# Four splits and four gate products of a state-space output, issued slot by slot

## The chip, the cores and the metric

The kernel runs on one core of a Trainium2 chip. The metric is the time of one execution on the device in microseconds (us), taken as the median over runs; beside it stands the profile of one execution, from which all rows below come.

## The reference

Two layers of a decoder trunk are applied to an input of 512 tokens by 1024 channels, in float32. In each layer the normalised input `h` goes through one large projection whose columns feed three token mixers, their gates and three merge gates. What matters here is the third mixer, a state-space model (SSM) over 512 channels, whose output `y` passes a gated linear unit and is multiplied with its own gate:

```python
h = rmsnorm(x, norm_g)
proj = h @ w_in
...
y = jax.nn.gelu(y)
y_ssm = y * jax.nn.sigmoid(y @ w_glu + b_glu)
...
y_c = y_ssm * jax.nn.silu(cz)
merged = sigmoid(ga) * (y_a @ proj_a) + sigmoid(gb) * (y_b @ proj_b) + sigmoid(gc) * (y_c @ proj_c)
x = x + merged @ w_out
```

## The kernel before, in words

**Three products for one.** The large matrix products are made with operands split in two: `split` (L280) lets ScalarE round a float32 tile to the matmul type (`h`, line L284) and VectorE subtract that from the original to give the low half (`l`). `three` issues high by high, high by low and low by high, and sums them in PSUM. Weights are treated alike: class `Weights` loads units of 128 by 1024 from HBM on the SP queue (`raw`, L308); `make` rounds a unit on ScalarE (`wh`, L318) and makes its low half on VectorE (`wl`). Raw units and both halves share twelve tiles, so a new half waits until TensorE or VectorE has let an older tile go.

**Slots.** The order of the work is a list of pieces, `ORDER`; each is one slot, and `now` counts them. A piece of a token-major product (`rq`, `rk`, `rv0`, `rv1`) is 24 matmuls for 128 tokens that use four weight units in turn, six matmuls a unit; four pieces share the four units. Other work is written as generators that yield the number of slots until their next step. In each slot the program issues the steps that are due, then the piece's matmuls, then steps that asked to come behind them, and then `W.fill()`, which makes the next weight units as tiles allow. After the last piece of a token-major product it makes four units at once. Every engine runs its own instructions in the order in which they were issued.

**Around the change.** The generator `ssm(q)` computes one quarter of the SSM's output, tile `y`, kept as `g[q]`. When the fourth quarter is done, in the third of the four pieces of `rv0`, it waits one slot and then splits all four tiles: four roundings `gh` on ScalarE and four subtractions `gl` on VectorE, in the slot of the last piece of `rv0`. Two slots later (`K["s7"]`) GpSimd multiplies each tile in place with the gate `zc`, named `silu` in the trace. The halves are read by the stage `glu`, which comes right after `rv1`; its evacuation multiplies the tiles, by then multiplied with the gate, with the sigmoid. The other names in the rows: `rv` (L1167) are the evacuations of `rv0` and `rv1`, one per piece; `rT` (L1160) copies a transposed piece of `rk` out of PSUM; `m` are the rotary products of `rk`; `kts` is the retention mixer's first work on GpSimd after `rv1`.

```python
            if q == 3:
                yield 1
                for i in range(4):
                    gs[i] = split(g[i], "g")
                yield K["s7"]
                for i in range(4):
                    while zc[i] is None:
                        yield 1
                    GT(out=g[i], in0=g[i], in1=zc[i], op=ALU.mult)
```

Of the kernel before, what the change touches and what calls it, by code (L numbers as in the profile page):

```python
# [14 lines left out]
ALU = mybir.AluOpType  # L15
# [20 lines left out]
K = dict(  # L36

    nw=12, w=4, raw=4, b=48,

    sb0=0, sb_gap=4, ssm0=6, ssm_gap=3, ret0=9, ret_gap=3, x0=-3, x1=2, ret_pre=4, lead=9,  # L40

    g=0.9, v=0.7,

    n1=1, n2=1, q1=1, q2=1, k1=1, k2=2, s1=1, s2=1, s3=1, s4=2, s5=1, s6=1, s7=2, b1=1, b2=1, b3=1,
# [142 lines left out]
def trunk(ctx: ExitStack, tc, x_in, w_in, par_in, bc_in, ng_in, cst_in, rope_in, out):  # L187
# [3 lines left out]
    def counted(f, engine, each):  # L191


        def g(*a, **k):
            o = k["out"] if "out" in k else a[0]
            load[engine] += 0.07 * (engine != "T") + each * math.prod(o.shape[1:])
            return f(*a, **k)  # L197

        return g
# [4 lines left out]
    GT, GS = counted(nc.gpsimd.tensor_tensor, "G", 2.2e-3), counted(nc.gpsimd.tensor_scalar, "G", 1.2e-3)  # L204
# [11 lines left out]
    def bt(name, dt=F32, shape=(P, 512)):  # L216
        return bp.tile(list(shape), dt, tag="b", name=name)
# [7 lines left out]
    def psm(name):  # L225
        return ps_sm.tile([P, 512], F32, tag="sm", name=name)
# [14 lines left out]
    def C(n):  # L241
# [7 lines left out]
        out=negm, in_=negm, pattern=[[1, P]], base=0, channel_multiplier=-1, compare_op=ALU.is_ge, fill=0.0  # L249
# [31 lines left out]
    def split(src, name, shape=(P, 512)):  # L281
        h = bt(name + "h", F32R, shape)
        l = bt(name + "l", F32R, shape)
        ACT(h, src, AF.Copy)  # L284
        TT(out=l, in0=src, in1=h.bitcast(F32), op=ALU.subtract)
        return h, l
# [108 lines left out]
    def transposed(src):  # L395
        pt = psm("T4")
        for i in range(4):
            nc.tensor.transpose(pt[:, i * P : i * P + P], src[:, i * P : i * P + P], ident)  # L398
        return pt
# [235 lines left out]
    def v3(ap, n=32):  # L635
        return ap.rearrange("p (g m) -> p g m", m=n)
# [173 lines left out]
    def layer(l, last, base):  # L810
# [59 lines left out]
        g = [None] * 4  # L870

        def ssm(q):
            win, ca, mt, T = coef.q[q]
            p0 = G * l + 8 * q

            pu = transposed(U[q])
            yield 0
            ut = bt("ut")
            for k in range(2):
                src = pu[64 * k : 64 * k + 64].rearrange("p (i c j) -> p i c j", i=4, j=2)  # L880
                for j in range(2):
                    dst = ut[64 * j : 64 * j + 64].rearrange("p (i k c) -> p i k c", i=4, k=2)
                    ACT(dst[:, :, k, :], src[:, :, :, j], AF.Copy)
            yield K["s1"]
            ps = psm("S")
            for n in range(8):
                sl = slice(n * 64, n * 64 + 64)
                MM(ps[:, sl], win[n // 4][:, n % 4 * P : n % 4 * P + P], ut[:, sl], start=True, stop=True)
            yield 0

            H, tm, tx = bt("H"), bt("tm"), bt("tx")
            lo, hi = slice(0, 64), slice(64, P)
            TT(out=tm, in0=ps, in1=T[0], op=ALU.mult)
            TT(out=tx[lo], in0=ps[hi], in1=T[1][hi], op=ALU.mult)
            TT(out=tx[hi], in0=ps[lo], in1=T[1][lo], op=ALU.mult)
            yield K["s2"]
            TT(out=tm, in0=tm, in1=tx, op=ALU.add)
            for n in range(8):
                sl = slice(n * 64, n * 64 + 64)
                nc.vector.tensor_tensor_scan(  # L900
                    tm[:, sl], r8[:, p0 + n : p0 + n + 1].to_broadcast([P, 64]), tm[:, sl], 0.0, ALU.mult, ALU.add
                )
            nc.gpsimd.memset(v3(H, 64)[:, :, 0:1], 0.0)
            yield K["s3"]

            def sh0(ap):
                return v3(ap, 64)[:, :, 0:63]

            def sh1(ap):
                return v3(ap, 64)[:, :, 1:64]  # L910


            TT(out=sh1(H), in0=sh0(tm), in1=sh0(T[0]), op=ALU.mult)
            TT(out=sh0(tx)[lo], in0=sh0(tm)[hi], in1=sh0(T[1])[hi], op=ALU.mult)
            TT(out=sh0(tx)[hi], in0=sh0(tm)[lo], in1=sh0(T[1])[lo], op=ALU.mult)
            TT(out=sh1(H), in0=sh1(H), in1=sh0(tx), op=ALU.subtract)
            yield K["s4"]

            py = psm("py")
            for i in range(4):  # L920

                for part in range(2):
                    for n in (i, i + 4):
                        sl = slice(n * 64, n * 64 + 64)
                        o = py[64 * (n // 4) : 64 * (n // 4) + 64, n % 4 * P : n % 4 * P + P]
                        k = 2 * (n % 2) + n // 4
                        if part == 0:
                            MM(o, ut[:, sl], mt[n % 4 // 2][:, k * P : k * P + P], start=True, stop=False)
                        else:
                            MM(o, H[:, sl], ca[:, n, 1:9, :].rearrange("p a b -> p (a b)"), start=False, stop=True)  # L930
            coef.used = q + 1
            yield 0
            ysb = bt("ysb")
            ACT(
                ysb.rearrange("p (j g m) -> p g j m", j=8, g=4), py.rearrange("p (g j m) -> p g j m", g=4, j=8), AF.Copy
            )
            yield K["s5"]
            pt = transposed(ysb)
            yield 0
            y = bt("y")  # L940
            for k in range(2):
                src = pt[64 * k : 64 * k + 64].rearrange("p (i h c) -> p i h c", i=4, h=2)
                for h in range(2):
                    dst = y[64 * h : 64 * h + 64].rearrange("p (c i k) -> p i c k", i=4, k=2)
                    ACT(dst[:, :, :, k], src[:, :, h, :], AF.Copy)

            u, sg = bt("gu"), bt("gs")
            ACT(u, y, AF.Square, scale=math.sqrt(0.044715))
            yield K["s6"]
            STT(out=u, in0=u, scalar=1.0, in1=y, op0=ALU.add, op1=ALU.mult)  # L950
            yield 0
            ACT(sg, u, AF.Sigmoid, scale=2.0 * math.sqrt(2.0 / math.pi))
            TT(out=y, in0=y, in1=sg, op=ALU.mult)
            g[q] = y
            if q == 3:
                yield 1
                for i in range(4):
                    gs[i] = split(g[i], "g")
                yield K["s7"]
                for i in range(4):  # L960
                    while zc[i] is None:
                        yield 1
                    GT(out=g[i], in0=g[i], in1=zc[i], op=ALU.mult)


        gs, yc, yb, mg, ya = [None] * 4, [None] * 4, [None] * 4, [None] * 8, [None] * 8
        zc, zb = [None] * 4, [None] * 4
# [349 lines left out]
        def quarters():  # L1317

            q = len(starts) - 1
            if q < 4 and coef.ready >= q and now[0] >= starts[-1]:  # L1320
                spawn(ssm(q), now[0])
                starts.append(now[0] + K["ssm_gap"])
# [15 lines left out]
        for name, m in mains:  # L1338
            i = now[0]
# [22 lines left out]
    while due:  # L1362
        i = min(due)
# [28 lines left out]
```

## Time and profile before

| what | value |
|---|---|
| median of 3 runs | 1310.49 us (1309.92 to 1311.5) |
| the profiled execution | 1311.17 us |
| its span, first to last instruction | 1309.5 us |
| TensorE busy | 97% |
| VectorE, ScalarE, GpSimd busy | 65%, 41%, 29% |
| mean granted clock of TensorE | 0.992 |

The profiled execution gives every duration and wait used below. PE is TensorE, DVE VectorE, ACT ScalarE, POOL GpSimd and SP the engine that issues the loads. Times in a timeline count from the start of the span. A matmul is pipelined: its row says 0.39 us, while the next starts 0.23 us after it.

### The profile page before, as it was taken

The numbers are of one execution on the slowest core, as the hardware profiler recorded it, in microseconds if no ns is written. First come the engines' busy times: TensorE is split into PE (matmuls) and PEld (weight loads), VectorE is DVE, ScalarE is ACT, GpSimd is POOL, SyncE is SP. The second block draws the span as 40 slices with busy tenths as digits, with TensorE's granted clock in tenths as the row PEclk, the third lists the DMA queues.
The fourth block names the chain that finished last, engine by engine and source line by source line (L and its number), as shares of the span: only waits on it lengthen the run. The fifth ranks groups of instructions, "written<-read, shape, count | busy, mean of one in ns | idle before, by whom it ended". The sixth has DMA issues, their size and how long they took to land. (4 is left out here: it accounts for less than half of the span.)

```text
span 1309.5 us, 16640 instructions
## 1 busy us (share of the span) xinstructions
PE 1271.7 (97%) x6360; PEld 1048.5 (80%) x6360; DVE 855.6 (65%) x1189; ACT 537.6 (41%) x919; POOL 382.5 (29%) x452
## 2 busy tenths in 40 slices
PE   6989989999999999999999999899999999999998
PEld 5867768788887888888888877788888878888887
DVE  5997678776785438556365576789657844575542
ACT  5445534445343534332244445344534534423311
POOL 3340036638442012000042000584555311210000
PEclk9989989999999999999999999899999999999999
DMA  6232221222322322234433222122241232222342
GB/s 223 90 124 77 65 65 49 81 81 89 119 68 65 104 77 77 81 97 141 161 118 127 81 65 71 43 81 65 84 127 65 65 120 90 65 74 88 97 135 75
DMA packets 37375, 120.05 MB, mean 92 GB/s; under 512 B 4144, under 2 KB 4528, under 8 KB 37296
## 3 DMA queue, kind: packets, MB, share of 16 engines
q1 hardware_dynamic: 29664, 105.40, 25.2%
q10 hardware_dynamic: 7632, 13.59, 3.1%
q8 instruction: 50, 0.82, 0.3%
q14 instruction: 29, 0.24, 0.1%
HBM read 114.78 MB, written 4.19 MB: 91 GB/s over the span
## 5 line engine op out<-in xcount | busy, mean ns | idle before, releaser
L197 DVE TENSOR_TENSOR wl<-raw,wh 128x1024 fp32r<-128x1024 f32 x196 | 251.6, 1294 | 114.6 <-ACT wh L318 111.8
L197 PE MATMUL mm<-hh,wh 128*128 128x512 f32 x640 | 256.0, 400 | 0.0
L197 PE MATMUL mm<-hh,wl 128*128 128x512 f32 x640 | 251.2, 393 | 4.9 <-DVE wl L197 4.9
L197 PE MATMUL mm<-hl,wh 128*128 128x512 f32 x640 | 250.7, 392 | 0.0
L318 ACT ACTIVATE wh<-raw 128x1024 fp32r<-128x1024 f32 x196 | 205.8, 1057 | 86.7 <-PE mm L197 38.9
L197 PE MATMUL mm<-wh,hh 128*128 128x512 f32 x512 | 207.5, 405 | 0.9 <-ACT hh L421 0.9
L197 PE MATMUL mm<-wl,hh 128*128 128x512 f32 x512 | 202.6, 396 | 4.3 <-DVE wl L197 4.3
L197 PE MATMUL mm<-wh,hl 128*128 128x512 f32 x512 | 202.0, 395 | 0.0
L197 PEld LDWEIGHTS mm<-hh,wl 128*128 128x128 f32 x640 | 120.8, 189 | 32.2 <-DVE wl L197 6.3
L197 PEld LDWEIGHTS mm<-hh,wh 128*128 128x128 f32 x640 | 121.0, 189 | 25.1 <-issue 1.6
L197 PEld LDWEIGHTS mm<-hl,wh 128*128 128x128 f32 x640 | 121.0, 189 | 23.5
L197 PEld LDWEIGHTS mm<-wl,hh 128*128 128x128 f32 x512 | 104.5, 204 | 24.5 <-DVE wl L197 7.8
L197 PEld LDWEIGHTS mm<-wh,hh 128*128 128x128 f32 x512 | 104.5, 204 | 19.0 <-ACT hh L421 1.3
L197 PEld LDWEIGHTS mm<-wh,hl 128*128 128x128 f32 x512 | 104.2, 204 | 18.4 <-DVE hl L197 0.3
L1051 DVE TENSOR_TENSOR_SCAN kp<-kp,zero 128x511 f32<-128x511 f32 (+1 forms) x64 | 67.6, 1076 | 26.2 <-ACT kp L1047 26.1
L994 ACT ACTIVATE gate<-mm 128x512 f32<-128x512 f32 x48 | 28.6, 596 | 114.2 <-PE mm L197 114.2
L197 POOL TENSOR_SCALAR ms<-ss 128x8 f32<-128x8 f32 (+3 forms) x56 | 19.1, 341 | 181.5 <-DVE ss L824 100.6
L197 POOL TENSOR_TENSOR rs<-ms,mhalf 128x8 f32<-128x8 f32 (+3 forms) x56 | 64.6, 1154 | 4.7
L1033 POOL CAST qd<-qd 64x512 fp32r<-64x512 f32 x16 | 16.3, 1016 | 134.1 <-ACT qd L1028 133.7
L822 ACT ACTIVATE sq<-mm 128x512 f32<-128x512 f32 x32 | 19.0, 593 | 84.6 <-PE mm L197 84.5
L197 PE MATMUL mm<-wl,mgh 128*128 128x512 f32 x128 | 50.1, 391 | 0.2
L197 PE MATMUL mm<-wh,mgh 128*128 128x512 f32 x128 | 49.9, 390 | 0.0
(253 smaller groups left out, 2263.2 us busy)
## 6 DMA issues: line engine op xcount, KB each, us to landing
raw<-in_w SPq DMA_DIRECT2D x196, 512.0 KB, 3.5
x<-in_x SPq DMA_DIRECT2D x8, 256.0 KB, 7.3
rope<-in_rope ACTq DMA_DIRECT2D x8, 256.0 KB, 3.7
xh<-in_x ACTq DMA_DIRECT2D x8, 256.0 KB, 4.4
x<-xh ACTq DMA_DIRECT2D x8, 256.0 KB, 2.0
xh<-x ACTq DMA_DIRECT2D x8, 256.0 KB, 4.6
out<-xh ACTq DMA_DIRECT2D x8, 256.0 KB, 2.1
gB<-in_ng SPq DMA_DIRECT2D x2, 256.0 KB, 5.8
```

Of the source, the lines that this page charges most:

```text
L197: return f(*a, **k)
L318: ACT(wh, raw, AF.Copy)
L822: ACT(s2, ps, AF.Square)
L994: ACT(sg, ps, AF.Sigmoid)
L1033: nc.gpsimd.tensor_copy(out=qd[h][o, :], in_=qd[h][r, :])
L1051: nc.vector.tensor_tensor_scan(v, v, zero1.to_broadcast([P, n - 1]), 1.0, ALU.mult, ALU.add)
```

## The change

In each layer, the split of one tile and the product of the tile before it go together into one slot: the first split where all four stood, then a split and a product in each of the next three slots, and the last product a slot later.

```diff
--- before.py
+++ after.py
@@ -953,14 +953,15 @@
             TT(out=y, in0=y, in1=sg, op=ALU.mult)
             g[q] = y
             if q == 3:
+                for i in range(4):
+                    yield 1
+                    gs[i] = split(g[i], "g")
+                    if i:
+                        while zc[i - 1] is None:
+                            yield 1
+                        GT(out=g[i - 1], in0=g[i - 1], in1=zc[i - 1], op=ALU.mult)
                 yield 1
-                for i in range(4):
-                    gs[i] = split(g[i], "g")
-                yield K["s7"]
-                for i in range(4):
-                    while zc[i] is None:
-                        yield 1
-                    GT(out=g[i], in0=g[i], in1=zc[i], op=ALU.mult)
+                GT(out=g[3], in0=g[3], in1=zc[3], op=ALU.mult)
 
 
         gs, yc, yb, mg, ya = [None] * 4, [None] * 4, [None] * 4, [None] * 8, [None] * 8
```

On ScalarE, from the evacuation in the last piece of `rv0` on, in the first layer. Names carry their buffer numbers here, and in brackets stands what an instruction waits for: an engine, or `DMAHW` for a load. Line numbers behind the change are one higher in the new program. Before:

```order
L1167 ACTIVATE rv_3762<-mm_3733 128x512 [waits PE_49]
L284 ACTIVATE gh_3770<-y_2669 128x512
L284 ACTIVATE gh_3774<-y_2812 128x512 [waits Pool_49]
L284 ACTIVATE gh_3778<-y_3470 128x512
L284 ACTIVATE gh_3782<-y_3712 128x512 [waits DMAHW6_49,DVE_49]
L1160 ACTIVATE rT_3811<-T4_3765 128x512 [waits PE_49,Activation_49]
L318 ACTIVATE wh_3813<-raw_3578 128x1024 [waits DMAHW5_49,PE_49]
L318 ACTIVATE wh_3819<-raw_3584 128x1024 [waits DMAHW6_49,PE_49]
L318 ACTIVATE wh_3825<-raw_3590 128x1024 [waits DMAHW7_49,PE_49]
L318 ACTIVATE wh_3831<-raw_3596 128x1024 [waits DMAHW0_49,DVE_49]
L1167 ACTIVATE rv_3837<-mm_3786 128x512 [waits PE_49]
L1160 ACTIVATE rT_3870<-T4_3840 128x512 [waits PE_49]
```

All four `gh` stand ahead of the four `wh`. With the change:

```order
L1168 ACTIVATE rv_3762<-mm_3733 128x512 [waits PE_49]
L284 ACTIVATE gh_3770<-y_2669 128x512
L1161 ACTIVATE rT_3799<-T4_3765 128x512 [waits PE_49,Pool_49]
L318 ACTIVATE wh_3801<-raw_3578 128x1024 [waits DMAHW5_49,PE_49]
L318 ACTIVATE wh_3807<-raw_3584 128x1024 [waits DMAHW6_49,PE_49]
L318 ACTIVATE wh_3813<-raw_3590 128x1024 [waits DMAHW7_49,PE_49]
L318 ACTIVATE wh_3819<-raw_3596 128x1024 [waits DMAHW0_49,PE_49]
L1168 ACTIVATE rv_3825<-mm_3774 128x512
L284 ACTIVATE gh_3833<-y_2812 128x512
L1161 ACTIVATE rT_3863<-T4_3828 128x512 [waits PE_49]
L1168 ACTIVATE rv_3865<-mm_3838 128x512 [waits PE_49,Pool_49]
L284 ACTIVATE gh_3873<-y_3470 128x512 [waits Activation_49]
```

Three of the four `gh` moved behind the four `wh`, one each between an evacuation of `rv` and the copy `rT`; the fourth `wh` waits for PE where it waited for DVE.

On VectorE, in the same place. Before:

```order
L197 TENSOR_TENSOR m_3632<-m_3632,m_3633 128x512
L197 TENSOR_TENSOR gl<-y,gh 128x512 x4
L197 TENSOR_TENSOR wl<-raw,wh 128x1024 x4
L197 TENSOR_TENSOR m_3676<-m_3676,m_3677 128x512
L197 TENSOR_TENSOR m_3728<-m_3728,m_3729 128x512
```

All four `gl` stand ahead of the four `wl`. With the change:

```order
L197 TENSOR_TENSOR m_3632<-m_3632,m_3633 128x512
L197 TENSOR_TENSOR gl<-y,gh 128x512
L197 TENSOR_TENSOR wl<-raw,wh 128x1024 x4
L197 TENSOR_TENSOR m_3676<-m_3676,m_3677 128x512
L197 TENSOR_TENSOR gl<-y,gh 128x512
L197 TENSOR_TENSOR m_3728<-m_3728,m_3729 128x512
L197 TENSOR_TENSOR gl<-y,gh 128x512 x2
```

One `gl` stays ahead of the four `wl`, and three come behind them, the last two in one row since nothing else is issued between. The order of GpSimd's instructions, of TensorE's and of the loads is the same in both programs, but for buffer numbers.

## Rows read from the trace of the kernel before

**Rows 1.** The page's head: the span, and TensorE's busy time and instructions.

```profile
span 1309.5 us, 16640 instructions
PE 1271.7 (97%) x6360; PEld 1048.5 (80%) x6360; DVE 855.6 (65%) x1189; ACT 537.6 (41%) x919; POOL 382.5 (29%) x452
```

**Rows 2.** TensorE's waits: whole run; 400 to 600 us; 600 to 800 us (total, times, longest).

```profile
PE mm L197 <- DVE wl L197: 9.2, 7, 3.3
...
PE mm L197 <- DVE wl L197: 2.1, 2, 1.6
...
PE wt L1068 <- DVE w L197: 1.3, 2, 0.7
```

**Rows 3.** Busy times by stretch: length, then each engine's; PEclk is the granted clock.

```profile
401.95:407.88 5.93, 5.93 (x32) 4.90 (x30) 4.94 (x5) 5.29 (x9) 4.17 (x3) 1.00 0.32 97
407.88:416.49 8.61, 6.49 (x32) 4.81 (x29) 7.77 (x6) 2.80 (x5) 3.12 (x2) 1.00 0.44 135
...
1043.99:1049.91 5.92, 5.92 (x31) 4.89 (x30) 4.93 (x5) 5.28 (x9) 4.16 (x3) 1.00 0.27 89
1049.91:1058.52 8.61, 6.48 (x31) 4.80 (x30) 7.78 (x6) 2.79 (x5) 3.13 (x2) 1.00 0.46 139
```

**Rows 4.** TensorE's timeline, first piece of `rv1`: start, length, instruction [idle before, releaser].

```profile
407.88 0.48 PE L197 MATMUL mm<-wh,hh 128*128 128x512 f32 x1
409.91 0.50 PE L197 MATMUL mm<-wl,hh 128*128 128x512 f32 x1 [1.56 <-DVE wl L197]
...
410.95 0.40 PE L197 MATMUL mm<-wh,hl 128*128 128x512 f32 x1
411.18 0.40 PE L197 MATMUL mm<-wh,hh 128*128 128x512 f32 x1
412.14 0.50 PE L197 MATMUL mm<-wl,hh 128*128 128x512 f32 x1 [0.56 <-DVE wl L197]
...
416.49 0.48 PE L197 MATMUL mm<-wh,hh 128*128 128x512 f32 x1
```

**Rows 5.** ScalarE's timeline, 402 to 413 us.

```profile
402.29 2.18 ACT L284 ACTIVATE gh<-y 128x512 fp32r<-128x512 f32 x4
404.37 0.58 ACT L1160 ACTIVATE rT<-T 128x512 f32<-128x512 f32 x1
404.85 1.05 ACT L318 ACTIVATE wh<-raw 128x1024 fp32r<-128x1024 f32 x1
...
412.12 1.06 ACT L318 ACTIVATE wh<-raw 128x1024 fp32r<-128x1024 f32 x1 [3.57 <-DVE wl L197]
```

**Rows 6.** VectorE's timeline, 402 to 413 us.

```profile
402.94 4.70 DVE L197 TENSOR_TENSOR gl<-y,gh 128x512 fp32r<-128x512 f32 x4 [3.71 <-ACT gh L284]
...
407.56 2.30 DVE L197 TENSOR_TENSOR wl<-raw,wh 128x1024 fp32r<-128x1024 f32 x1
...
409.78 2.30 DVE L197 TENSOR_TENSOR wl<-raw,wh 128x1024 fp32r<-128x1024 f32 x1
...
412.01 1.21 DVE L197 TENSOR_TENSOR wl<-raw,wh 128x1024 fp32r<-128x1024 f32 x1
```

**Rows 7.** GpSimd's timeline, 402 to 455 us: the products, and what follows them.

```profile
403.71 7.29 POOL L197 TENSOR_TENSOR y<-y,silu 128x512 f32<-128x512 f32 x4 [8.29 <-DVE gl L197]
453.95 0.74 POOL L197 TENSOR_TENSOR kts<-m,kts 128x256 fp32r<-128x256 f32 x1 [42.95 <-ACT kts L290]
```

**Rows 8.** ScalarE's and VectorE's timelines, 422 to 432 us.

```profile
422.32 0.60 ACT L1167 ACTIVATE rv<-mm 128x512 f32<-128x512 f32 x1 [4.84 <-PE mm L197]
...
428.18 0.60 ACT L1167 ACTIVATE rv<-mm 128x512 f32<-128x512 f32 x1 [4.77 <-PE mm L197]
429.31 1.06 ACT L318 ACTIVATE wh<-raw 128x1024 fp32r<-128x1024 f32 x1 [0.54 <-PE mm L197]
...
430.41 1.23 DVE L197 TENSOR_TENSOR wl<-raw,wh 128x1024 fp32r<-128x1024 f32 x1 [14.67 <-ACT wh L318]
```

**Rows 9.** The matmuls that read `gh`, both layers: durations, first and last start.

```profile
L197 PE MATMUL mm<-gh,wh x32: 389/389/389, 433.4 to 1085.7; 128*128 128x512 f32 x32
```

## The prediction

> **What bounds the kernel now.** I read the page first: TensorE is busy for 1271.7 of 1309.5 us [rows 1], so the time can only fall where TensorE stands still. The list of TensorE's waits names such places [rows 2]. Over the whole run it waits 9.2 us, in 7 waits, for `wl`, the low half of a weight unit that VectorE makes. Two of the 7 lie between 400 and 600 us, cost 2.1 us together and are the only waits of that stretch; between 1000 and 1310 us the list answers with the same line, word for word. From 600 to 800 us there is only 1.3 us, for the stick-breaking weights of the second layer.
>
> The place is the first piece of `rv1`. A piece of a token-major product is 24 matmuls and one small transpose, and its length shows in the busy times by stretch [rows 3]: the piece before takes 5.93 us, this one 8.61 us, with TensorE busy for 6.49 us only. The second layer repeats it: 5.92 and 8.61 us. The granted clock is 1.00 in all four, so the difference is waiting alone.
>
> TensorE's timeline shows it by matmul [rows 4]: the first matmul of the piece starts at 407.88 us, its second, which wants `wl` of the first weight unit, at 409.91, after 1.56 us of idle time. The eighth, which wants `wl` of the second unit, starts 0.96 us after the seventh, where the sixth and the seventh are 0.23 us apart. The next piece begins at 416.49.
>
> Why is `wl` late? The timelines of the three other engines tell it. ScalarE rounds the four `y` tiles one after the other in 2.18 us, then copies one transpose, and only then rounds the first two weight units, at 404.85 us [rows 5]. VectorE makes the four low halves `gl` in 4.70 us, up to 407.64, and then the first `wl`, from 407.56 to 409.86 [rows 6]. So the rounded first unit, ready at 405.90, lies for 1.7 us while VectorE is still at `gl`. VectorE is slow there as well: the first `wl` and the second take 2.30 us each, the third 1.21 us. GpSimd's four products with the gate run from 403.71 to 411.00 [rows 7], beside the slow instructions and not beside the third.
>
> **The change, part by part.** Nothing is removed or added: four roundings, four subtractions and four products move to other slots, in each of two layers. No DMA is issued by them; the orders of TensorE, GpSimd and SP stay as they were, but for names.
>
> *Three roundings leave ScalarE's queue ahead of the weights.* Their spacing is (2.18 − 0.62) / 3 = 0.52 us, so `wh` may begin 1.56 us sooner: 403.3 us instead of 404.85 [rows 5]. It also needs the tile of an earlier weight unit, which TensorE lets go after a quarter of the piece that began at 401.95: 401.95 + 5.93/4 = 403.4. I take 403.4. The bounds are 403.3 and the old 404.85.
>
> *Three subtractions leave VectorE's queue ahead of the weights.* `gl` of the first tile ends at 403.63 and the first `wl` is next. The new queue then runs, with a rounding at 1.05 us [rows 5] and units let go at each further quarter of the piece (404.9, 406.4, 407.9): `wh` ready at 404.5, 406.0, 407.5, 408.9. The first product still runs from 403.7 to 405.4, so I give the first `wl` its largest length, 2.30 us, and the others 1.23. The low halves are then ready at 406.8, 408.0, 409.3, 410.5. TensorE starts the piece at 407.88 as before and wants them at 408.2, 409.6, 411.0, 412.3 (six matmuls of 0.23 us for a unit). All four come 1.4 us or more ahead: no wait is left.
>
> *The other bound.* Suppose ScalarE gains nothing and the first `wl` starts at 405.9 and takes 2.30 us: 408.2, just in time, and the rest follow 1.23 us apart. Only if the second also took 2.30 us would it come at 410.5, 0.9 us late.
>
> At this point a rule may be weighed against the rows. By the Trainium skill (SBUF — State Buffer, "Who interferes with whom") a VectorE instruction with two inputs in SBUF and a GpSimd instruction that reads SBUF block each other for a whole instruction, whichever comes second. The long `gl` and `wl` beside the products agree [rows 6, 7]; by that rule the first `wl` would stand until 405.39 and end at 406.6, where the row's length gives 406.8, and the sum would be the same. By the same rule the products, once they stand singly, can each hold up another VectorE instruction; what that would cost here is the second form of the first rival.
>
> *The fourth rounding of the batch* waited 3.57 us for VectorE's second `wl` and started at 412.12 [rows 5]. In the new program it waits for TensorE instead, because the tiles fall in another order; the estimate above has it done at 408.9. If it were still to wait for the second `wl`, at 408.0, it would be no later.
>
> *The moved work in its new slots* costs nothing that I can find. ScalarE is idle for 4.84 and 4.77 us before two of the evacuations of `rv` [rows 8], and each slot gets one rounding of 0.62 us. VectorE idles 14.67 us before the weights of the `glu` stage [rows 8], which takes three subtractions of 0.69 us. GpSimd's next work after the products comes 42.95 us later [rows 7]. If the cover were gone, each rounding would cost 0.52 us of ScalarE and each subtraction 0.69 us of VectorE. The first reader of the moved halves is the `glu` stage at 433.4 us [rows 9]; the last half, issued with the evacuation at 422.3 less the gain, is ready by about 421.5.
>
> *What is late next.* The weights of `glu` are rounded as TensorE lets tiles go (ScalarE waits 0.54 us for TensorE before the first [rows 8]), so they move forward with it. No wait of TensorE follows until the next layer, and there the waits start from TensorE's own scores.
>
> **The sum.** Piece 8.61 − 5.93 = 2.68 us, twice: 5.36 us. The profiled execution took 1311.17 us, of which 1309.5 is the span; it should become 1305.8 with a span of 1304.1. It lies 0.7 us above the median of the runs, 1310.49, so the predicted median is **1305.1 us**.
>
> **The rivals.**
>
> *Part of the wait stays.* The second `wl` is disturbed as well, or `wh` gains nothing: 0.9 us stays per layer, the gain is 2 × (2.68 − 0.9) = 3.5 us, 1307.0 us. For it: two `wl` took 2.30 us in the trace [rows 6]. Against it: the second product now stands behind the second `gl`, which VectorE issues after all four `wl`, so only the first product can disturb one.
>
> A second form of this rival follows from products that now run singly beside later VectorE work: one of 1.7 us [rows 7] that held back a `wl` of `glu` in full, in each layer, would leave 5.4 − 3.4 = 2.0 us, 1308.5 us. By the blocking rule of the same page of the Trainium skill (SBUF — State Buffer, "Who interferes with whom") that is what a meeting costs. The rows put the last product at about 421.5 to 423.2 and the `wl` at 427.7, 430.41 less 2.7, so they don't meet.
>
> *The gain is given back later.* TensorE comes 2.68 us earlier to `glu` or to the chunk products behind it and waits there for something that does not move with it: 1310.5 us, no change. For it: the low half of the first `glu` unit is ready at 431.6 [rows 8], only 1.8 us ahead of the stage's first matmul. Against it: that unit waits for TensorE itself, and GpSimd, the engine that would fall behind unseen, idles for 42.95 us.
>
> *Slower.* The last split now stands three pieces later. Its rounding is behind the evacuation of an earlier piece, and the evacuations in turn wait for tiles that the products set free; a product late by one piece would hold ScalarE, then the last split, and TensorE would wait at `glu`. The point from which this decides is the distance from 421.5 to TensorE's first read at 433.4 − 2.7 = 430.7, about 9 us; the fourth tile is read by the tenth matmul of `glu`, at 432.8, 11.3 us. If each of the three slots slid by a whole piece (3 × 5.93 = 17.8 us) the halves would come 6.5 us late, per layer 6.5 − 2.68 = 3.8 us more than before: 1318 us. Against it: a product takes 1.7 us [rows 7], and none waits for work of a later piece.
>
> That the change doesn't do what it says is excluded by the orders shown above: one split stands ahead of the weights where four stood.
>
> **How the numbers follow.** The forecast, both waits gone in both layers, gets 0.85; part of the wait 0.06, two thirds of it still over the bound; no change 0.05; slower 0.04. A measurement of this kernel can tell 0.2%, 2.6 us, from no change. Faster is 0.85 + 0.04 = 0.89, the same 0.02 + 0.05 = 0.07, slower 0.04. The range: the runs before span 1309.92 to 1311.5; less 5.36 that is 1304.6 to 1306.1. I add half a microsecond below for the median of other runs and reach above to the partial gain (1307.0 and the same half): 1304.0 to 1307.5. Left out are no change, slower and a little of the partial case, about 0.12.
>
> **What would show it.** In the profile after, the first piece of `rv1` takes 5.9 us in both layers and TensorE's idle time before `mm<-wl` there is gone; its waits for `wl` fall from 9.2 to about 5 us. The first `wl` starts near 404.5, the fourth ends near 410.5, the four products stand in four pieces. TensorE busy stays at 1271.7 us. The prediction is wrong if TensorE shows a new wait at `glu` or in the chunk products, or if the piece stays above 7 us.

## The result, and the profile after

| | before | with the change |
|---|---|---|
| median of 5 runs | 1310.25 us (1309.92 to 1311.5) | 1304.23 us (1303.71 to 1305.5) |
| ratio, 95% interval | | 0.9948 (0.9938 to 0.9959) |
| the profiled execution, its span | 1311.17 us, 1309.5 us | 1303.83 us, 1302.1 us |
| first piece of `rv1`, layer 1 and 2 | 8.61 and 8.62 us | 5.92 and 5.92 us |

The kernel is faster by more than 0.2%. The ratio says 6.8 us, with an interval of 5.4 to 8.1, and the two medians of the table differ by 6.0; 5.36 us were forecast. The same program, measured twice more below, gave 0.996 and 0.9959, which is 5.2 and 5.4 us.

The head of the page after the change [rows 1]:

```profile
span 1302.1 us, 16638 instructions
PE 1270.3 (98%) x6360; PEld 1049.2 (81%) x6360; DVE 850.1 (65%) x1189; ACT 537.7 (41%) x919; POOL 378.5 (29%) x452
```

TensorE has the same 6360 matmuls and is busy for 1.4 us less. The span fell by 7.4 us, so 6.0 us of it are time in which TensorE stood still. TensorE's waits over the whole run after the change [rows 2]; the columns are the total, the count and the longest:

```profile
PE wt L1069 <- DVE w L197: 13.2, 8, 3.1
PE T L398 <- DVE xn L197: 7.9, 2, 7.2
PE z L197 <- DVE ks L197: 3.1, 1, 3.1
PE mm L197 <- DVE wl L197: 2.2, 3, 0.8
```

Three waits for `wl` are left of seven, and none of them is at `rv1`. The busy times by stretch after the change [rows 3], for the last piece of `rv0` and the first of `rv1` in the first layer, and the first of `rv1` in the second:

```profile
400.64:406.57 5.93, 5.93 (x31) 4.90 (x30) 3.90 (x4) 4.78 (x7) 1.29 (x1) 1.00 0.32 98
406.57:412.49 5.92, 5.92 (x31) 4.89 (x30) 3.88 (x5) 2.49 (x5) 1.67 (x1) 1.00 0.81 259
...
1045.25:1051.17 5.92, 5.92 (x31) 4.89 (x30) 3.87 (x5) 2.49 (x5) 1.67 (x1) 1.00 0.76 264
```

The long piece is as short as its neighbours and TensorE is busy through all of it. How the weights come in time is seen on the other engines. The last piece of `rv0` began at 401.95 us before and begins at 400.64 here, so 1.31 us are to be added for a comparison with the old rows; a time so shifted is called old time below. ScalarE's timeline after the change [rows 5]:

```profile
400.98 0.62 ACT L284 ACTIVATE gh<-y 128x512 fp32r<-128x512 f32 x1
401.50 0.59 ACT L1161 ACTIVATE rT<-T 128x512 f32<-128x512 f32 x1
...
402.08 1.06 ACT L318 ACTIVATE wh<-raw 128x1024 fp32r<-128x1024 f32 x1
...
406.42 1.06 ACT L318 ACTIVATE wh<-raw 128x1024 fp32r<-128x1024 f32 x1 [0.30 <-PE mm L197]
```

VectorE's [rows 6]:

```profile
401.63 0.69 DVE L197 TENSOR_TENSOR gl<-y,gh 128x512 fp32r<-128x512 f32 x1 [3.71 <-ACT gh L284]
...
403.18 1.61 DVE L197 TENSOR_TENSOR wl<-raw,wh 128x1024 fp32r<-128x1024 f32 x1 [0.85 <-ACT wh L318]
...
404.87 1.23 DVE L197 TENSOR_TENSOR wl<-raw,wh 128x1024 fp32r<-128x1024 f32 x1
...
407.51 1.23 DVE L197 TENSOR_TENSOR wl<-raw,wh 128x1024 fp32r<-128x1024 f32 x1
...
419.55 0.69 DVE L197 TENSOR_TENSOR gl<-y,gh 128x512 fp32r<-128x512 f32 x1 [5.30 <-ACT gh L284]
```

And GpSimd's [rows 7]:

```profile
402.41 1.29 POOL L197 TENSOR_TENSOR y<-y,silu 128x512 f32<-128x512 f32 x1 [8.29 <-DVE gl L197]
410.02 1.67 POOL L197 TENSOR_TENSOR y<-y,silu 128x512 f32<-128x512 f32 x1 [6.32 <-DVE gl L197]
414.39 1.30 POOL L197 TENSOR_TENSOR y<-y,silu 128x512 f32<-128x512 f32 x1 [2.70 <-DVE gl L197]
420.39 1.29 POOL L197 TENSOR_TENSOR y<-y,silu 128x512 f32<-128x512 f32 x1 [4.70 <-DVE gl L197]
```

The first `wl` starts at 403.18, in old time 404.49 instead of 407.56, and the last ends at 408.74, in old time 410.05 instead of 414.54. Only the first product meets a `wl`; the others run alone or beside one rotary sum.

### The profile page after: what moved, and what is told of

It is laid out like the page before. It is cut to its first block, busy times and chain, and to the rows that moved or that the text cites. A ratio compares the mean times of both kernels' runs of the same rounds, so it can differ in the third digit from the quotient of the medians.

```text
span 1302.1 us, 16638 instructions
## 1 busy us (share of the span) xinstructions
PE 1270.3 (98%) x6360; PEld 1049.2 (81%) x6360; DVE 850.1 (65%) x1189; ACT 537.7 (41%) x919; POOL 378.5 (29%) x452
## 5 line engine op out<-in xcount | busy, mean ns | idle before, releaser
L197 DVE TENSOR_TENSOR wl<-raw,wh 128x1024 fp32r<-128x1024 f32 x196 | 247.9, 1272 | 99.9 <-ACT wh L318 96.6
```

## The experiments

The theory after the result was the prediction's own (A): two waits per layer vanish, 5.4 us, and the rest of the first ratio is something in which two executions of one program differ. Its rival (B) was that the changed program gains another 0.7 to 1.4 us somewhere. Side by side stood the question which half of the edit does it, and why.

**The kernel before, again** (no edit).

> The kernel before, unchanged, once more. Theory A (the change gains the two waits at rv1 and nothing else; what went beyond 5.36 us is how the stretches at half clock and the start fall in one execution): ratio 1.000 within its interval; the first piece of rv1 takes 8.6 us in both layers; but the positions of TensorE up to 400 us differ from the first profile by some tenths to over 1 us. Theory B (the extra 0.7 to 1.4 us belongs to the changed program): the start and the stick-breaking stages repeat the first profile within 0.2 us.

Measured: 1310.46 us, ratio 0.9998 (0.9989 to 1.0007). The last piece of `rv0` and the first of `rv1`:

```profile
402.96:408.89 5.93, 5.93 (x32) 4.90 (x30) 4.94 (x5) 5.29 (x9) 4.17 (x3) 1.00 0.32 93
408.89:417.51 8.62, 6.49 (x32) 4.82 (x30) 7.77 (x6) 2.80 (x5) 3.12 (x2) 1.00 0.47 143
```

The wait is there again, to 0.01 us. But the piece begins 1.0 us later than in the first profile, for the same program. That is theory A's sign: the way to that point differs from execution to execution.

**The change, again** (no further edit).

> The changed kernel once more. Theory A: 5.4 us less than before on the mean of many rounds, ratio about 0.9959; pieces of 5.93 us; the rest of the difference between profiles changes in size from one profile to the next. Theory B: 6.0 us or more again, ratio 0.9954 or less, with the same places as in the first profile of the change (up to 200 us, and 834 us).

Measured: 1305.69 us, ratio 0.996 (0.9947 to 0.9972), 5.2 us. The pieces take 5.92 and 5.92 us. The last piece of `rv0` begins at 402.83 us; in the first profile of the very same program it began at 400.64. So 2.2 us of difference arise ahead of the change, and theory B falls as far as the start is concerned. At 834 us a gain came back, of another size: see the table of all profiles below.

**Only the splits spread.**

```diff
+                for i in range(4):
+                    yield 1
+                    gs[i] = split(g[i], "g")
                 yield 1
-                for i in range(4):
-                    gs[i] = split(g[i], "g")
-                yield K["s7"]
                 for i in range(4):
-                    while zc[i] is None:
-                        yield 1
                     GT(out=g[i], in0=g[i], in1=zc[i], op=ALU.mult)
```

> Only the four splits are spread over slots; the four products are issued together a slot after the last split. GpSimd's order of instructions is that of before and of the change. Theory A: the same as the change, 5.4 us below before, first piece of rv1 5.93 us, since a product starts when its split is done, in whatever slot it was issued. Rival (the spacing of the products matters): part of the wait stays, 1 to 4 us gained.

Measured: 1305.37 us, ratio 0.996 (0.9947 to 0.9972). The first piece of `rv1`:

```profile
407.20:413.12 5.92, 5.92 (x31) 4.89 (x30) 3.87 (x5) 2.49 (x5) 1.67 (x1) 1.00 0.81 260
```

All of the gain, as A had it. GpSimd is busy in that stretch for the same 1.67 us as with the full change: a product follows its split, whatever slot it was issued in.

**Only the products spread.**

```diff
                 for i in range(4):
                     gs[i] = split(g[i], "g")
-                yield K["s7"]
                 for i in range(4):
-                    while zc[i] is None:
-                        yield 1
+                    yield 1
                     GT(out=g[i], in0=g[i], in1=zc[i], op=ALU.mult)
```

> Only the four products are spread over slots; the four splits stay together ahead of the weights. Theory A: no change, within 0.1% of before, first piece of rv1 8.6 us, since GpSimd has nothing else to do and starts each product when its subtraction is done. Rival (spreading the products takes them off VectorE's weights): first piece of rv1 about 5.9 to 7 us, 3 to 5 us gained.

Measured: 1311.55 us, ratio 1.0006 (0.9997 to 1.0015).

```profile
408.62:417.24 8.62, 6.49 (x32) 4.82 (x30) 7.78 (x6) 2.81 (x5) 3.13 (x2) 1.00 0.44 137
```

Nothing changes. Issued in other slots, the products do not move in time as long as the splits stay; when the splits move, they carry the products along.

**The splits together, the products truly held back.** A copy of one column, which must wait for the evacuation of the first piece of `rv1`, stands ahead of the products on GpSimd.

```diff
                 yield K["s7"]
+                nc.gpsimd.tensor_copy(out=sg[:, 0:1], in_=rv[0][1][:, 0:1])
                 for i in range(4):
-                    while zc[i] is None:
-                        yield 1
                     GT(out=g[i], in0=g[i], in1=zc[i], op=ALU.mult)
```

> The four splits stay together ahead of the weights as before; GpSimd's products are held back by a copy of one column of rv, which is evacuated after the first piece of rv1, so that no product runs beside gl or wl. Theory C (the splits ahead of the weights do harm only together with the products beside them): gl takes 2.5 us in place of 4.7, the first wl starts at 406.0 on the clock of the first profile and all wl take 1.2 us, the first piece of rv1 takes 5.9 us, gain 5 to 6 us as the change. Rival D (three splits ahead of the weights are late by themselves): the piece stays above 7 us, gain under 3 us.

Measured: 1305.74 us, ratio 0.9961 (0.9947 to 0.9975). The first piece of `rv1`, then VectorE's timeline:

```profile
408.37:414.29 5.92, 5.92 (x31) 4.89 (x30) 4.08 (x5) 2.81 (x5) 0.00 (x0) 1.00 0.80 241
```

```profile
403.43 2.50 DVE L197 TENSOR_TENSOR gl<-y,gh 128x512 fp32r<-128x512 f32 x4 [3.71 <-ACT gh L284]
406.42 2.36 DVE L197 TENSOR_TENSOR wl<-raw,wh 128x1024 fp32r<-128x1024 f32 x2 [0.49 <-ACT wh L318]
409.07 2.54 DVE L197 TENSOR_TENSOR wl<-raw,wh 128x1024 fp32r<-128x1024 f32 x2 [0.29 <-ACT wh L318]
```

The whole gain without moving a split. Four `gl` ahead of the weights take 2.50 us instead of 4.70 [rows 6] and do no harm. So theory C holds and rival D falls: the splits ahead of the weights made TensorE wait only because GpSimd's products ran beside the splits and the first weights.

**The splits spread, other work of GpSimd beside the weights.**

```diff
                     gs[i] = split(g[i], "g")
+                    if i == 0:
+                        for n in range(4):
+                            nc.gpsimd.tensor_tensor(out=u, in0=gs[0][1].bitcast(F32), in1=sg, op=ALU.mult)
```

(on top of the version with only the splits spread)

> The splits are spread as in the change, but GpSimd makes four more multiplications (low half of the first tile by the finished sigmoid tile, into a tile that nobody reads) right after the first subtraction, beside the four wl. This work is added and its result not used. Theory C: the first three wl take 2.3 us each, but start at 403 to 404.5, so that they come at about the time they are wanted; the first piece of rv1 takes 5.9 to 6.6 us, gain 4 to 6 us. Rival E (the neighbourhood of products and wl alone makes the wait): the piece takes 8 us or more, gain under 1.5 us.

Measured: 1308.74 us, ratio 0.9982 (0.9973 to 0.9991). The first piece of `rv1`, VectorE's four `wl`, and the last three of GpSimd's added multiplications:

```profile
407.79:414.94 7.15, 6.41 (x31) 4.74 (x30) 6.97 (x6) 3.04 (x6) 5.99 (x3) 1.00 0.61 181
```

```profile
404.39 1.61 DVE L197 TENSOR_TENSOR wl<-raw,wh 128x1024 fp32r<-128x1024 f32 x1 [0.85 <-ACT wh L318]
...
406.09 2.15 DVE L197 TENSOR_TENSOR wl<-raw,wh 128x1024 fp32r<-128x1024 f32 x1
...
408.33 2.15 DVE L197 TENSOR_TENSOR wl<-raw,wh 128x1024 fp32r<-128x1024 f32 x1
...
410.57 2.14 DVE L197 TENSOR_TENSOR wl<-raw,wh 128x1024 fp32r<-128x1024 f32 x1
```

```profile
405.00 2.16 POOL L961 TENSOR_TENSOR gu<-gl,gs 128x512 f32<-128x512 f32 x1
...
407.23 2.16 POOL L961 TENSOR_TENSOR gu<-gl,gs 128x512 f32<-128x512 f32 x1
...
409.47 2.16 POOL L961 TENSOR_TENSOR gu<-gl,gs 128x512 f32<-128x512 f32 x1
```

Between the two expectations: the piece takes 7.15 us, above the 5.9 to 6.6 of theory C and well below the 8 of rival E. The gain is about 2.4 us. With the splits spread, GpSimd's work beside the weights makes something less than half of the old wait: 7.15 − 5.93 = 1.22 of 2.68 us. The added work is not the old one: it lies beside all four `wl`, where the products lay beside two. TensorE stands twice in the piece:

```profile
412.76 0.50 PE L197 MATMUL mm<-wl,hh 128*128 128x512 f32 x1 [0.38 <-DVE wl L197]
...
414.56 0.30 PE L398 MATMUL T<-ident,m 128*128 128x128 f32 x1 [0.36 <-DVE m L197]
```

The last `wl` ends at 412.7, where TensorE wanted it 4.4 us into the piece, at 412.2. The other half of the wait is the transpose at the end of the piece: it reads the rotary product `m`, which VectorE makes behind the four `wl`.

**The change in one layer alone.** The new lines stand under `if l == 0:` (or `l == 1`), the old ones under `else:`.

> The change in the first layer only. Theory F (the 2.7 us gained in the first layer move the second layer's stick-breaking wait against the points at which TensorE's clock falls to the lower level, so fewer matmuls run there): first piece of rv1 5.93 us in layer 1, 8.6 in layer 2, and TensorE's way from 824 to 836 us takes 11.5 to 11.8 us, not 12.0 to 12.1; gain 2.7 + 0.3 to 0.6 = 3.0 to 3.3 us. Rival (that gain is chance): 12.0 to 12.1 us there, gain 2.7 us.

> The change in the second layer only. Theory F: 8.6 us for the piece in layer 1, 5.93 in layer 2; from 824 to 836 us 12.0 to 12.1 us as before, since nothing ahead of it moved; gain 2.7 us and no more. Rival (the gain at 830 us comes from elsewhere in the changed program): 11.5 to 11.8 us here as well.

Measured: layer 1 alone 1307.92 us, ratio 0.9976 (0.9965 to 0.9987); layer 2 alone 1307.33 us, ratio 0.9971 (0.9959 to 0.9982). The two ratios, 3.1 and 3.8 us, cannot be told apart; the second lies above the 2.7 us that theory F gave it, with an interval of 2.4 to 5.4. The profiles say more. Theory F is about a wait of two parts, 3.30 and 2.71 us from matmul to matmul, in which TensorE stands for the second layer's stick-breaking weights; its granted clock falls to the lower level, 0.50, within that wait and in eleven of the twelve profiles rises 6.8 us later. Busy times by stretch, first from the start of the wait to the fall of the clock, then at the lower level, in the first profile of before:

```profile
824.64:828.10 3.46, 0.39 (x3) 0.23 (x2) 3.36 (x3) 2.26 (x4) 3.46 (x3) 1.00 0.49 152
828.10:834.93 6.83, 4.42 (x16) 3.83 (x16) 6.53 (x6) 0.98 (x2) 3.74 (x4) 0.50 0.10 27
```

and of the change:

```profile
820.59:822.81 2.22, 0.23 (x2) 0.10 (x1) 2.12 (x2) 2.22 (x4) 2.22 (x2) 1.00 0.71 210
822.81:829.64 6.83, 3.49 (x13) 3.06 (x14) 6.63 (x6) 1.02 (x3) 4.98 (x5) 0.50 0.02 8
```

The clock falls 2.22 us into the wait instead of 3.46, so more of the slow stretch lies in the wait and fewer matmuls, 13 instead of 16, run in it. All profiles together, with the time from one and the same matmul (at 824.0 us in the first profile) to another (at 836.0), worked out from their start times:

| profile | first piece of `rv1`, layers 1 and 2 | fall of the clock after the wait's start | 824 to 836 us |
|---|---|---|---|
| splits only | 5.92, 5.92 | 2.17 | 11.48 |
| the change, first | 5.92, 5.92 | 2.22 | 11.50 |
| products held | 5.92, 5.92 | 2.76 | 11.75 |
| the change, again | 5.92, 5.92 | 2.81 | 11.77 |
| the change, third | 5.92, 5.92 | 2.94 | 11.83 |
| layer 1 alone | 5.92, 8.62 | 3.08 | 11.88 |
| layer 2 alone | 8.60, 5.92 | 3.35 | 12.01 |
| before, again | 8.62, 8.62 | 3.36 | 12.02 |
| before, first | 8.61, 8.62 | 3.46 | 12.06 |
| products only | 8.62, 8.61 | 3.62 | 12.14 |
| other work beside | 7.15, 7.14 | 4.62 | 12.58 |
| the further step (next experiment) | 5.92, 5.92 | 5.54 | 11.46 |

In the first eleven profiles the length of the stretch follows the place of the fall, 0.45 us for each microsecond. With the first layer's gain of 2.7 us the fall came early in six of them, and without it late in all four; a gain of 1.5 us made it later still. The twelfth profile, of the further step below, has the first layer's gain and a late fall, but there the clock rose again after 3.4 us, and the stretch is the shortest of all. So in all seven profiles with the gain of 2.7 us the stretch took at most 11.88 us, and in the four without it at least 12.01. Layer 1 alone gave 11.88, between what theory F and its rival said (11.5 to 11.8, and 12.0 to 12.1), layer 2 alone 12.01 as theory F said; these two profiles by themselves differ by 0.13 us, less than the 0.33 us between the three of the change. It is the order of all profiles that ties the effect to the shift of the first layer. Its size, 0.15 to 0.6 us here, changes between executions of one program. Why the clock falls where it falls was not tried.

**A further step in the same manner, beside the change a third time.**

```diff
-            spawn(within(), now[0] + K["w2"])
+            spawn(within(), now[0] + K["w2"] + (q == 0))
```

> The change, and in it the step that makes the inner-block matrix of the SSM's first quarter (VectorE's kk, 1.45 us) one slot later, so that it stands behind the four wl of that slot and not ahead of them. Theory G (small VectorE work ahead of a batch of wl is what makes TensorE wait, there as at rv1): TensorE's step of 1.19 us at 223 us in the profile of the change, and its twin in the second layer, fall to 0.23; 1.9 us below the change, ratio to before 0.9945. Rival (something else behind it is late by then, or the later matrix holds up the SSM): no gain or a new wait after 225 us.

> The changed kernel a third time, beside the one above. Theory A with theory F: ratio to before 0.9955 to 0.996, that is 5.4 us for the two waits and 0.2 to 0.6 us for the later fall of the clock in the second layer.

Measured: with the further step 1304.28 us, ratio 0.9955 (0.9942 to 0.9967); the change a third time 1305.64 us, ratio 0.9959 (0.9946 to 0.9973). The two cannot be told apart. TensorE's waits from 215 to 235 us, with the further step:

```profile
PE wt L1069 <- DVE w L197: 0.8, 1, 0.8
PE mm L197 <- DVE wl L197: 0.5, 1, 0.5
```

With the change alone there is one wait there, 0.8 us for `wl`. The step took 0.3 us off it and added 0.8 us for the stick-breaking weights `w`. From 200 to 400 us TensorE took 199.95 us with the change and 199.96 with the step, and from 836 to 1040 us, in the second layer, 203.93 in both. Theory G, as a rule that moving a little VectorE work always pays, falls: here the wait changed its name. The timelines show where the time went. With the change alone, `w`, the first `wl`, and GpSimd:

```profile
221.18 0.42 DVE L197 TENSOR_TENSOR w<-w,kp 128x255 f32<-128x255 f32 x1
222.85 1.22 DVE L197 TENSOR_TENSOR wl<-raw,wh 128x1024 fp32r<-128x1024 f32 x1
223.00 6.47 POOL L801 COPY mt<-kk 32x256 f32<-32x256 f32 x8 [2.46 <-DVE kk L197]
```

And with the further step:

```profile
221.20 1.03 DVE L197 TENSOR_TENSOR w<-w,kp 128x255 f32<-128x255 f32 x1
222.16 2.29 DVE L197 TENSOR_TENSOR wl<-raw,wh 128x1024 fp32r<-128x1024 f32 x1
220.52 1.44 POOL L197 TENSOR_TENSOR ct<-bbi,y_im 128x512 f32<-128x512 f32 x1
222.04 1.33 POOL L197 TENSOR_TENSOR ab<-ab,ct 128x512 f32<-128x512 f32 x1
```

In the change GpSimd stands for 2.46 us until `kk` is made. With `kk` made later it goes on with its own products, and `w` and the first `wl` beside them take 1.03 and 2.29 us instead of 0.42 and 1.22: the same meeting as at `rv1`. That this and nothing else ate the gain was not tried.

## Why the prediction was right or wrong

**The place and the size of the waits: right; the cause: right in part.** The first piece of `rv1` went from 8.61 and 8.62 to 5.92 us, 2.69 + 2.70 = 5.39 us where the sum had 5.36. The working held step by step, in old time: the first `wh` starts at 403.39 (403.4 was taken), the four `wl` are ready at 406.1, 407.4, 408.7 and 410.05 (406.8, 408.0, 409.3, 410.5), the fourth `wh` is done at 408.8 (408.9), the last `gl` at 421.55 (421.5). The first `wl` took 1.61 us, not the 2.30 assumed, which was the safe side. But the working credits the gain to the shorter queues ahead of the weights, and took GpSimd's products in only as a length of `wl`. The run with the products held shows that the full queue costs nothing without them: the piece takes 5.92 us there too.

**The step that failed: the sum, and the width put around it.** "The sum" counted the two waits and nothing else. The second layer's wait at 824 us was put at nothing because "there the waits start from TensorE's own scores". It did move along, but the fall of the clock within it did not keep its place, and the stretch of 12.06 us took 11.50 us in the first profile of the change, 11.77 and 11.83 in the two others. The term that was left out measured 0.56, 0.29 and 0.23 us. It depends on the shift: it cost 0.5 us in the run with a shift of 1.5 us.

The range allowed "half a microsecond below for the median of other runs". The ratio of 0.9948, put to the 1310.49 us that were shown, gives 1303.7 us, below the 1304.0 of the range, and the gain of 6.8 us is 1.4 above the forecast. Of these, some 0.2 to 0.6 are the missing term. The rest was not found in the program: two more measurements gave 0.996 and 0.9959, or 5.2 and 5.4 us, and between the first profiles of before and after the 7.4 us of span are the two waits (5.39), the term left out (0.56), 1.31 us that arise ahead of the change, and 0.1 us. TensorE reached the last piece of `rv0`, ahead of which nothing was changed, at 400.64, 402.83 and 403.44 us in three executions of the changed program, and at 401.95 and 402.96 in two of before. That the first ratio came out so far from the sum is therefore chance in the main; its interval, 5.4 to 8.1 us, holds the sum with the missing term. The range should have taken the width of two medians, one on either side of the comparison, and not half of one.

**The rivals.** None of the wait stayed. The nearest to the first rival is the run with other work beside, where all four `wl` were long: the piece took 7.15 us, 1.2 us of wait where the rival had 0.9. The gain was not given back later: between 424 and 800, between 872 and 1040, and between 1060 and 1240 us the way of TensorE from a matmul to the same matmul is equal to 0.1 us in before and after. The slower case stayed far: `glu` reads its first half at 429.4 us, and the last half is ready at 420.24, a distance of 9.2 us where about 9 were forecast. The second form, a product in the way of a `wl` of `glu`, did not arise: the last product ends at 421.7, the `wl` starts at 426.4.

**The weighed rule.** In the rows after, the first product ends at 403.70, and the `wl` that had started at 403.18 ends 1.09 us after it; alone it takes 1.23. The run with other work beside shows turns: the second multiplication ends at 407.16, the `wl` beside it at 408.24, the next multiplication at 409.39, the next `wl` at 410.48. By the Trainium skill (SBUF — State Buffer, "Who interferes with whom") a VectorE instruction with two inputs in SBUF and a GpSimd instruction that reads SBUF shut each other out, and the second stands for the whole length of the first. The rows agree to about 0.3 us: a turn of both took 2.24 us, where the two lengths alone, 1.23 and 1.29, add up to 2.52.

**Smaller claims.** The waits for `wl` fell to 2.2 us, not about 5: near 90 us TensorE waits twice, for `ks` and for `wl`, 0.8 and 3.3 us in the first profile of before, 4.1 and 1.0 in the second, 3.1 and 0.6 after, so the sum by name changes between executions of one program. TensorE's busy time fell by 1.4 us where it was to stay. Of this 1.1 us lie in the two long pieces themselves, with 6.49 and 6.48 us of busy time before [rows 3] and 5.92 after; from 824 to 836 us, where fewer matmuls ran at the lower clock, it fell by another 0.4 us. A product takes 1.29 us alone; the 1.7 us of the forecast was a length beside VectorE's work.

## What to carry to other kernels

What stands ahead of a batch that the bound engine waits for is to be priced at the length that it has beside its neighbours: four subtractions cost 4.70 us beside GpSimd's products and 2.50 us alone. Taking away the neighbour was enough here; spreading the queue was enough too, but it took the products along, and with other GpSimd work in their place 1.22 of 2.68 us of wait stayed. Check whether moving an instruction in the program moves it in time: spreading the products did nothing, since each one follows its input. And when the forecast is a few tenths of a per cent, take the spread of the start into the range on both sides of the comparison.

## What the runs showed of the hardware

Two things were not expected. VectorE's subtraction and GpSimd's multiplication, both with work queued, take turns in the run with other work beside, and the profile books the waiting as length: 1.23 us becomes 2.15 us and 1.29 us becomes 2.16 us, with no idle time shown (subtractions of 128 by 1024, products of 128 by 512). And in 12 profiles the same wait of TensorE saw its clock fall between 2.17 and 5.54 us after the wait's start, with 6.8 us at the lower level in eleven and 3.4 us in one; the time of the same matmuls lay between 11.46 and 12.58 us.
